# Four-model block on one core: softmax of negated scores with fewer reciprocals, and latent-attention queries of 96 columns a head

## The chip, the cores and the metric

The kernel runs on one core of a Trainium2 chip. The metric is device time in microseconds for one launch, which computes a whole stack of layers for 512 tokens of width 1024. The times of the kernel before are 1867.73, 1868.81 and 1868.92 us, median 1868.81 us.

## The reference, cut to what matters

Two blocks run one after the other. The first has a sparse-attention mixer (8 heads), a gated linear mixer and a feed-forward part. The second has four layers, each followed by a layer norm: latent attention (`_mla_branch`), sliding-window attention, attention with a forget gate (`_fox_branch`), and latent attention once more. The change touches the dense causal softmax, which the sparse mixer, the forget-gate layer and both latent layers use, and the queries and keys of the two latent layers:

```python
q = (_rmsnorm(cq, q_norm) @ w_q_up).reshape(B, S, 16, 64 + 32)
kv = (_rmsnorm(ckv, kv_norm) @ w_kv_up).reshape(B, S, 16, 64 + 64)
q_rope = _apply_rope(q[..., 64:], cos, sin)   # [x1*cos - x2*sin, x2*cos + x1*sin], halves of 16
k_rope = _apply_rope(k_rope, cos, sin)        # one, shared by all 16 heads
q_full = concat([q[..., :64], q_rope]);  k_full = concat([kv[..., :64], k_rope])
s = einsum(q_blk, k_full) * 96 ** -0.5;  s = where(causal, s, -1e30)
p = softmax(s);  o = einsum(p, v)             # swept over 128-query blocks
```

## The kernel before

Everything is computed in fp32 accuracy by splitting each operand into a high part (fp32r, made by ScalarE) and a low part (the rest, made by VectorE); a product of two split operands is three matmuls on TensorE: high by high, high by low and low by high (`mm3`, lines 268 to 277). The Python code is traced by a framework that then orders the instructions of each engine itself, by a simulated timeline and the buffers that its pools have: the program text sets what is computed and which buffers there are, and each engine then runs its own list strictly in order.

A latent layer (`mla`, from line 1107) first projects the tokens to the low-rank vectors (`cq`, 384 wide, and `ckv`, 256 wide) and transposes them to feature-major tiles `ct`. It then loops over four quads of four heads. For a quad it loads and splits the query weights, the key and value weights and the gate weights, projects the gates (`pj<-Ah,wh` in the rows) and the values (`vt`, four token blocks), and then takes two pairs of heads. For a pair it projects the keys of both heads at once (a matmul group with 128 features and 512 tokens, `pj<-cth,wh`), splits each half into the tiles `k4h` and `k4l`, and projects each head's query in a group of its own, again of 128 features: 64 plain features, 32 rotary ones, and the same 32 once more with the two halves swapped, so that the rotation needs one multiplication by a table (`tab`, line 1204) whose rows hold cos, cos, -sin, sin; the sum over features then adds the products. The keys carry the rotated key on both sets of 32 rows. The three matmuls of each of a query projection's three feature chunks are nine matmuls of 512 columns. The query is then split into `qh` (ScalarE, line 218) and `ql` (VectorE, line 219), both of which read the projection's PSUM bank `pj`. There are three such banks, two `s` banks for scores and two `t` banks for transposes.

`dense_head` (line 316) takes the four query blocks of a head. For each block TensorE makes the scores; VectorE adds the mask and takes the row maximum in one instruction (L324), negates it (L326, one column); ScalarE takes the exponential and the row sum (L327); VectorE takes the reciprocal (L328, one column) and scales the block (L331). TensorE then transposes the blocks (L337), ScalarE copies the transposes out (`pt`, L205), and `dense_values` multiplies them with the values of both heads of the pair into the one bank `o` (L350), which VectorE multiplies by the gate into `og` (L1103). `og` has eight tiles of 512 columns, two a quad.

In the rows `wl<-wr,wh` and `wh<-wr` are weight splits, `sp` the scores, `mx` and `nm` the maximum and its negative, `sum` and `rc` the row sum and its reciprocal. VectorE is DVE, ScalarE is ACT, GpSimd POOL, SyncE SP; TensorE is PE, its weight loads PEld.

## Time and profile before

| what | value |
|---|---|
| median of three runs | 1868.81 us |
| the profiled execution: its own time, and its span from first to last instruction | 1871.75 us, 1870.0 us |
| granted TensorE clock, mean | 0.997 |
| TensorE, VectorE, ScalarE busy share | 97%, 65%, 49% |
| first latent layer, four quads (890 to 1064 us) | 174 us |
| second latent layer, four quads (1655 to 1830 us) | 175 us |
| forget-gate layer, four quads (1350 to 1573 us) | 223 us |

The busy time of a matmul in the rows contains its way through the array, so that neighbours overlap; what a matmul costs in a dense row is the distance from its start to the next one's. A bracket at the end of a row gives the idle time of the engine just before it and what ended it.

### The profile page before, as it was taken

How to read it: one execution, taken by the hardware profiler on the slowest of the kernel's cores; microseconds unless marked ns; L12 is line 12 of the kernel's file. 1: busy time of each engine (PE TensorE's matmuls, PEld its weight loads, DVE VectorE, ACT ScalarE, POOL GpSimd, SP SyncE). 2: the span in 40 equal slices, each digit the busy share in tenths (PEclk: the TensorE clock that was granted, in tenths of full speed). 3: DMA queues.
4: the chain of work that ended last, by engine and by line, in shares of the span. 5: the costliest groups of instructions: out<-in, count | busy, mean ns of one | idle time of the engine just before them, and what ended most of it. 6: DMA issues, size and time to landing. Idle time of an engine off the chain costs nothing.

```text
span 1870.0 us, 27371 instructions
## 1 busy us (share of the span) xinstructions
PE 1822.0 (97%) x10155; PEld 1498.8 (80%) x10155; DVE 1223.9 (65%) x3055; ACT 907.1 (49%) x2030; POOL 166.6 (9%) x217
## 2 busy tenths in 40 slices
PE   7999999999999999999999999999999999999997
PEld 7877777678888888879887788877888877988775
DVE  5554387754954664556878675576776666787866
ACT  4543336743442442344667434463566564366651
POOL 2211200000200000001000011241000000200001
PEclk9999999999999999999999999999999999999999
DMA  7222141042332342324221133221432322232111
GB/s 217 80 58 57 36 127 40 26 139 79 91 106 75 102 132 81 91 76 108 58 71 57 47 104 91 70 64 38 113 80 54 83 69 79 75 87 59 47 56 46
DMA packets 200752, 148.14 MB, mean 79 GB/s; under 512 B 8765, under 2 KB 178538, under 8 KB 200618
## 3 DMA queue, kind: packets, MB, share of 16 engines
q1 hardware_dynamic: 198826, 140.97, 26.3%
q0 software_dynamic: 1792, 5.42, 0.9%
q8 instruction: 80, 1.31, 0.3%
q14 instruction: 54, 0.44, 0.1%
HBM read 144.27 MB, written 2.10 MB: 78 GB/s over the span
## 4 chain that ended last, share of the span: by engine, by line
PE 67%; DVE 4%; ACT 2%; issue 1%; POOL 0%; POOLq 0%; DVEq 0%; ACTq 0%
PE pj L273 17%; PE pj L275 17%; PE pj L276 16%; PE o L350 3%; PE pj L937 3%; PE t L337 3%; PE s L937 1%; DVE wl L215 1%; PE s L275 1%; PE s L273 1%; PE s L276 1%; PE t L937 1%; PE t L372 1%; PE t L1319 1%; PE s L1419 1%
## 5 line engine op out<-in xcount | busy, mean ns | idle before, releaser
L214 ACT ACTIVATE wh<-wr 128x1024 fp32r<-128x1024 f32 (+10 forms) x408 | 296.0, 755 | 408.7 <-PE pj L275 130.9
L215 DVE TENSOR_TENSOR wl<-wr,wh 128x1024 fp32r<-128x1024 f32 (+10 forms) x408 | 344.0, 866 | 215.2 <-ACT wh L214 210.5
L273 PE MATMUL pj<-Ah,wh 128*128 128x512 f32 (+1 forms) x944 | 370.6, 393 | 4.8 <-DVE fg L288 2.8
L275 PE MATMUL pj<-Al,wh 128*128 128x512 f32 (+1 forms) x944 | 369.0, 391 | 0.2 <-DVE Al L215 0.2
L276 PE MATMUL pj<-Ah,wl 128*128 128x512 f32 (+1 forms) x944 | 368.1, 391 | 0.0
L273 PE MATMUL pj<-wh,Ah 128*128 128x512 f32 (+5 forms) x640 | 219.0, 343 | 4.7 <-ACT Ah L214 4.6
L275 PE MATMUL pj<-wl,Ah 128*128 128x512 f32 (+5 forms) x640 | 216.6, 339 | 0.0
L276 PE MATMUL pj<-wh,Al 128*128 128x512 f32 (+5 forms) x640 | 214.8, 340 | 0.5 <-DVE Al L215 0.4
L273 PEld LDWEIGHTS pj<-Ah,wh 128*128 128x128 f32 x944 | 178.1, 189 | 42.4 <-DVE fg L288 3.2
L276 PEld LDWEIGHTS pj<-Ah,wl 128*128 128x128 f32 x944 | 178.2, 189 | 37.4 <-issue 1.5
L275 PEld LDWEIGHTS pj<-Al,wh 128*128 128x128 f32 x944 | 178.1, 189 | 35.6 <-issue 0.8
L327 ACT ACTIVATE sp<-sp,nm 128x128 f32<-128x128 f32 (+3 forms) x256 | 142.8, 559 | 75.5 <-DVE nm L326 73.4
L205 ACT ACTIVATE pt<-t 128x512 f32<-128x512 f32 (+3 forms) x288 | 115.1, 444 | 106.1 <-PE t L337 66.8
L324 DVE CUSTOM_DVE_ANT_0 sp<-s,c_causal 128x128 f32<-128x128 f32 (+3 forms) x256 | 121.1, 486 | 56.7 <-PE s L276 23.5
L273 PEld LDWEIGHTS pj<-wh,Ah 128*128 128x128 f32 x640 | 121.4, 190 | 19.6 <-ACT Ah L214 7.3
L276 PEld LDWEIGHTS pj<-wh,Al 128*128 128x128 f32 x640 | 120.9, 190 | 12.6 <-DVE Al L215 1.6
L275 PEld LDWEIGHTS pj<-wl,Ah 128*128 128x128 f32 x640 | 121.5, 190 | 10.9 <-issue 0.2
L337 PE MATMUL t<-ident,sp 128*128 128x128 f32 x640 | 108.9, 278 | 5.1 <-ACT pt L205 5.0
L337 PEld LDWEIGHTS t<-ident,sp 128*128 128x128 f32 x640 | 77.3, 140 | 30.8 <-ACT pt L205 12.7
L331 DVE TENSOR_SCALAR sp<-sp,rc 128x128 f32<-128x128 f32 (+3 forms) x256 | 96.7, 383 | 5.0
L273 PE MATMUL pj<-wh,hdh 128*128 128x512 f32 x176 | 69.1, 393 | 3.3 <-ACT fg L205 2.2
L275 PE MATMUL pj<-wl,hdh 128*128 128x512 f32 x176 | 68.6, 390 | 0.0
(474 smaller groups left out, 3304.4 us busy)
## 6 DMA issues: line engine op xcount, KB each, us to landing
wr<-in_w_in_dram SPq DMA_DIRECT2D x34, 512.0 KB, 3.9
wr<-in_fox_w_in_dram SPq DMA_DIRECT2D x30, 512.0 KB, 4.1
wr<-in_w_ffn_gate_dram SPq DMA_DIRECT2D x22, 512.0 KB, 4.2
wr<-in_w_ffn_up_dram SPq DMA_DIRECT2D x22, 512.0 KB, 3.8
wr<-in_w_ffn_down_dram SPq DMA_DIRECT2D x22, 512.0 KB, 3.6
wr<-in_swa_w_in_dram SPq DMA_DIRECT2D x20, 512.0 KB, 3.8
wr<-in_mla_w_in_dram SPq DMA_DIRECT2D x16, 512.0 KB, 4.0
wr<-in_mla_w_out_dram SPq DMA_DIRECT2D x16, 512.0 KB, 3.8
```

Of the source, the lines that this page charges most:

```text
L205: return self.nc.scalar.activation(out, in_, AF.Copy, scale=1.0 if scale is None else scale)
L214: self.nc.scalar.activation(h, src, AF.Copy)
L215: self.nc.vector.tensor_tensor(out=l, in0=src, in1=h.bitcast(F32), op=ALU.subtract)
L273: mm = self.nc.tensor.matmul(ps, lhsT=ah, rhs=bh, start=i == 0, stop=False)
L275: self.nc.tensor.matmul(ps, lhsT=ah, rhs=bl, start=False, stop=False)
L276: mm = self.nc.tensor.matmul(ps, lhsT=al, rhs=bh, start=False, stop=i == n - 1)
L324: nc.vector.tensor_tensor_reduce(out=v, in0=ps, in1=self.causal[:, S - n:S], scale=1.0, scalar=LOWEST, op0=ALU.add, op1=ALU.max, accum_out ...
L327: nc.scalar.activation(v, v, AF.Exp, bias=nm[:, g], accum_out=sm[:, g])
L331: nc.vector.tensor_scalar(v, v, rc[:, g], None, ALU.mult)
L337: nc.tensor.transpose(ps[:, (b - j) * 128:(b - j + 1) * 128], sp[:, POFF[b] + j * 128:POFF[b] + j * 128 + 128], self.ident)
L350: mm = self.nc.tensor.matmul(po[64 * i:64 * i + 64, j * 128:S], lhsT=value(j, i), rhs=pt[:, TOFF[j]:TOFF[j] + (NB - j) * 128], start=first ...
L937: nc.tensor.matmul(ps, lhsT=x, rhs=y, start=first and k == 0 and i == 0, stop=last and k == 3 and i == 2, skip_group_check=True)
```

## The change

In `dense_head` the instruction that masks the scores now writes their negative and takes the row minimum, so that the negated maximum comes out of it directly and the separate negation goes; the exponential gets a scale of -1. The reciprocals of the first three blocks are taken in one instruction of three columns after the third block's row sum is there, and their three scalings follow it; the fourth block has its own.

In `mla` a quad's queries now take three projections of 128 features, where they took four. The first two, one for each head of the first pair, hold that head's 64 plain features, its 32 rotary features, and the 32 rotary features of the head at the same place in the second pair. The third holds the plain features of both heads of the second pair. No feature is projected twice: a query's rotary features x enter the scores as x cos and x sin, 32 rows each, and the keys carry the rotated key on the first 32 and its swapped and signed form on the second 32. For a head of the first pair VectorE therefore makes four products on 32 rows each out of the projection (new line 1221): two into a tile `qf` for the head of the second pair, two in place in the bank. For the second pair ScalarE copies the plain features into `qf`, and the split reads `qf`. `qf` lies in tiles 6 and 7 of `og` in the first three quads; in the fourth it is a third tile of the two-buffer pool `vt`. The query weights of a quad come in seven column ranges in place of two, and are split by two wide instructions on each of ScalarE and VectorE in place of fourteen narrow ones.

```diff
@@ dense_head
             nc.vector.tensor_tensor_reduce(
-                out=v, in0=ps, in1=self.causal[:, S - n:S], scale=1.0, scalar=LOWEST, op0=ALU.add, op1=ALU.max, accum_out=mx[:, g])
-            nc.vector.tensor_scalar(nm[:, g], mx[:, g], -1.0, None, ALU.mult)
-            nc.scalar.activation(v, v, AF.Exp, bias=nm[:, g], accum_out=sm[:, g])
+                out=v, in0=ps, in1=self.causal[:, S - n:S], scale=-1.0, scalar=-LOWEST, op0=ALU.add, op1=ALU.min, accum_out=nm[:, g])
+            nc.scalar.activation(v, v, AF.Exp, bias=nm[:, g], scale=-1.0, accum_out=sm[:, g])
+            if b < NB - 2:
+                continue
+
+            done = range(NB - 1) if b == NB - 2 else (b,)
+            g = slice(done[0], b + 1)
             nc.vector.reciprocal(rc[:, g], sm[:, g])
...
-            nc.vector.tensor_scalar(v, v, rc[:, g], None, ALU.mult)
+            for c in done:
+                v = sp[:, POFF[c]:POFF[c] + (c + 1) * 128]
+                nc.vector.tensor_scalar(v, v, rc[:, c:c + 1], None, ALU.mult)
@@ mla, keys: 32 + 32 rows, the second 32 swapped and signed
-                    for r0 in (0, 32, 64, 96):
-                        nc.vector.tensor_tensor(out=kr[:, b, r0:r0 + 32], in0=t[:, 0:32], in1=t[:, 32:64], op=ALU.add)
...
+                    nc.vector.tensor_tensor(out=kv[:, :, 0:32], in0=tv(0, 32), in1=tv(32, 32), op=ALU.add)
+                    nc.vector.tensor_tensor(out=kv[:, :, 32:48], in0=tv(16, 16), in1=tv(48, 16), op=ALU.add)
+                    nc.vector.scalar_tensor_tensor(out=kv[:, :, 48:64], in0=tv(0, 16), scalar=-1.0, in1=tv(32, 16), op0=ALU.mult, op1=ALU.subtract)
@@ mla, query weights
-                for pr in range(2):
-                    v = self.wload(wqu, 0, 3, (quad * 384 + pr * 192, 192))
-                    h, l = self.wtile(3, 256)
...
+                for ranges in (((0, 96), (256, 32), (160, 32), (352, 32), (96, 64)), ((192, 64), (288, 64))):
+                    v = self.wload(wqu, 0, 3, *((o + c, n) for c, n in ranges))
+                    h, l = self.wtile(3, v.shape[-1])
+                    self.split_into(h, l, v)
@@ mla, queries
+                    if pr == 0:
+                        room = og[:, KD - 2:KD] if quad < 3 else l2.tile([128, NB, 256], F32, name="vt").rearrange("p (h c) n -> p h (c n)", h=2)
+                        qf = [room[:, hh] for hh in range(2)]
+                    else:
+                        ps = self.pj()
+                        self.proj_feat(ps, qw[1], cq, kc=3)
+                        for hh in range(2):
+                            r = slice(64 * hh, 64 * hh + 64)
+                            self.acopy(qf[hh][r], ps[r], 96 ** -0.5)
                     for hh in range(2):
-                        ps = self.pj()
-                        self.proj_feat(ps, qw[pr], cq, kc=3, cols=slice(hh * 128, hh * 128 + 128))
-                        r = slice(64 - 64 * hh, 128 - 64 * hh)
-                        nc.vector.tensor_tensor(out=ps[r], in0=ps[r], in1=tab[r], op=ALU.mult)
                         q = [l2.tile([128, S], F32R, name=n) for n in ("qh", "ql")]
-                        self.split_gain(*q, ps, scale[:, hh:hh + 1])
+                        if pr == 0:
+                            ps = self.pj()
+                            self.proj_feat(ps, qw[0], cq, kc=3, cols=slice(hh * 128, hh * 128 + 128))
+                            own, other = (slice(64 - 64 * hh + c, 96 - 64 * hh + c) for c in (0, 32))
+                            for out, src, tab in ((qf[hh][own], other, cos), (qf[hh][other], other, sin), (ps[other], own, sin), (ps[own], own, cos)):
+                                nc.vector.tensor_tensor(out=out, in0=ps[src], in1=tab[src], op=ALU.mult)
+                            self.split_gain(*q, ps, scale[:, hh:hh + 1])
+                        else:
+                            self.split_into(*q, qf[hh])
```

Over the whole program this takes 72 matmuls of 512 columns from TensorE (24 of each of the three kinds). The framework orders all engines anew. Three places matter below.

**VectorE, first quad of the first latent layer**, from the first rotation on; `pj` here is the bank of a projection, `k4l` the low part of a key, `wl` a weight split for the next quad, `ql` the low part of the query. Before:

```order
L1204 TENSOR_TENSOR pj<-pj,c_mla_tab 64x512
L215 TENSOR_TENSOR k4l<-pj,k4h 64x512
L219 SCALAR_TENSOR_TENSOR ql<-pj,scale,qh 128x512
L1204 TENSOR_TENSOR pj<-pj,c_mla_tab 64x512
L215 TENSOR_TENSOR wl<-wr,wh 128x1024
L219 SCALAR_TENSOR_TENSOR ql<-pj,scale,qh 128x512
```

The first query's low part stands third in this list, the second query's sixth. The same place in the changed program:

```order
L1221 TENSOR_TENSOR og<-pj,c_mla_cos 32x512
L1221 TENSOR_TENSOR og<-pj,c_mla_sin 32x512
L211 TENSOR_TENSOR k4l<-pj,k4h 64x512
L1221 TENSOR_TENSOR pj<-pj,c_mla_sin 32x512
L1221 TENSOR_TENSOR og<-pj,c_mla_cos 32x512
L1221 TENSOR_TENSOR og<-pj,c_mla_sin 32x512
L1221 TENSOR_TENSOR pj<-pj,c_mla_cos 32x512
L211 TENSOR_TENSOR wl<-wr,wh 128x1024
L1221 TENSOR_TENSOR pj<-pj,c_mla_sin 32x512
L211 TENSOR_TENSOR wl<-wr,wh 128x1024
L211 TENSOR_TENSOR k4l<-pj,k4h 64x512
L215 SCALAR_TENSOR_TENSOR ql<-pj,scale,qh 128x512
```

The first query's low part now stands twelfth: seven of the eight products, both weight splits and two key splits are ahead of it.

**VectorE, second quad of the first latent layer**, between the second head's products and the first head's low part (`sp,nm<-s` is the masked minimum of a score block, the `nm` row under it reads its result out, `og<-o` is the gate of the pair before). Before, the matching place has one product for each head:

```order
L1204 TENSOR_TENSOR pj<-pj,c_mla_tab 64x512
L215 TENSOR_TENSOR k4l<-pj,k4h 64x512
L324 ISA sp,mx<-s,c_causal 128x256
L324 ISA mx 128x1
L219 SCALAR_TENSOR_TENSOR ql<-pj,scale,qh 128x512
```

After, the low part comes behind two more weight splits, a key split and the gate:

```order
L1221 TENSOR_TENSOR og<-pj,c_mla_sin 32x512
L321 ISA sp,nm<-s,c_causal 128x128
L321 ISA nm 128x1
L321 ISA sp,nm<-s,c_causal 128x256
L321 ISA nm 128x1
L1221 TENSOR_TENSOR pj<-pj,c_mla_cos 32x512
L211 TENSOR_TENSOR wl<-wr,wh 128x1024
L1221 TENSOR_TENSOR pj<-pj,c_mla_sin 32x512
L211 TENSOR_TENSOR wl<-wr,wh 128x1024
L211 TENSOR_TENSOR k4l<-pj,k4h 64x512
L1106 SCALAR_TENSOR_TENSOR og<-o,og 128x512
L215 SCALAR_TENSOR_TENSOR ql<-pj,scale,qh 128x512
```

Ahead of this piece stand three more products, the first two of either head's and one in the bank.

**VectorE, fourth quad of the first latent layer.** Before, its first rotation stands among the blocks of the third quad's last heads, 33 rows of the list ahead of the gate `og<-o` of the third quad's second pair:

```order
L215 TENSOR_TENSOR k4l<-pj,k4h 64x512
L1204 TENSOR_TENSOR pj<-pj,c_mla_tab 64x512
L215 TENSOR_TENSOR k4l<-pj,k4h 64x512
L324 ISA sp,mx<-s,c_causal 128x384
L324 ISA mx 128x1
```

After, all eight products follow that gate in one run, since `qf` is here a `vt` tile whose buffer the third quad's values hold until the matmuls of `o` have read them:

```order
L211 TENSOR_TENSOR k4l<-pj,k4h 64x512
L329 RECIPROCAL rc<-sum 128x1
L334 TENSOR_SCALAR sp<-sp,rc 128x512
L211 TENSOR_TENSOR wl<-wr,wh 128x1024
L1106 SCALAR_TENSOR_TENSOR og<-o,og 128x512
L1221 TENSOR_TENSOR vt<-pj,c_mla_cos 32x512
L1221 TENSOR_TENSOR vt<-pj,c_mla_sin 32x512
L1221 TENSOR_TENSOR vt<-pj,c_mla_cos 32x512
L1221 TENSOR_TENSOR vt<-pj,c_mla_sin 32x512
L1221 TENSOR_TENSOR pj<-pj,c_mla_sin 32x512 x2
L1221 TENSOR_TENSOR pj<-pj,c_mla_cos 32x512 x2
L215 SCALAR_TENSOR_TENSOR ql<-pj,scale,qh 128x512 x2
```

Both query projections of the fourth quad are made before that gate and hold two of the three `pj` banks until these rows are done.

## Rows read from the trace of the kernel before

**Rows 1.** Page: engine, busy us (share of the span) x instructions.
```profile
PE 1822.0 (97%) x10155; PEld 1498.8 (80%) x10155; DVE 1223.9 (65%) x3055; ACT 907.1 (49%) x2030; POOL 166.6 (9%) x217
```
**Rows 2.** Windows of the two latent layers' quads: width, PE, PEld, DVE, ACT busy.
```profile
890.00:1064.00 174.00, 171.86 (x951) 136.51 (x952) 135.12 (x447) 111.36 (x295) 1.15 (x2) 1.00 0.19 57
1655.00:1830.00 175.00, 172.23 (x952) 136.68 (x953) 135.48 (x447) 112.41 (x297) 1.15 (x2) 1.00 0.18 54
```
**Rows 3.** Timeline, first quad of the first latent layer: start us, us, instruction.
```profile
891.98 0.40 PE L273 MATMUL pj<-cth,wh 128*128 128x512 f32 x1
...
894.08 0.39 PE L273 MATMUL pj<-cth,wh 128*128 128x512 f32 x1
...
894.28 0.71 DVE L1204 TENSOR_TENSOR pj<-pj,c_mla_tab 64x512 f32<-64x512 f32 x1 [0.20 <-PE pj L276]
...
895.02 0.69 ACT L218 ACTIVATE qh<-pj,scale 128x512 fp32r<-128x512 f32 x1 [0.91 <-DVE pj L1204]
...
895.74 0.75 DVE L219 SCALAR_TENSOR_TENSOR ql<-pj,scale,qh 128x512 fp32r<-128x512 f32 x1
...
897.58 0.22 PE L273 MATMUL s<-k4h,qh 128*128 128x128 f32 x1
...
898.03 0.39 PE L276 MATMUL s<-k4h,ql 128*128 128x128 f32 x2
898.27 0.39 PE L273 MATMUL pj<-cth,wh 128*128 128x512 f32 x1
...
904.22 0.47 PE L273 MATMUL pj<-Ah,wh 128*128 128x512 f32 x1 [0.38 <-DVE k4l L215]
```
**Rows 4.** Groups by shape on DVE, 840 to 1095 us: busy, mean ns of one.
```profile
L215 DVE TENSOR_TENSOR wl<-wr,wh 128x1024 fp32r<-128x1024 f32 x19 | 23.0, 1217 | 1.9 <-ACT wh L214 1.7
L219 DVE SCALAR_TENSOR_TENSOR ql<-pj,scale,qh 128x512 fp32r<-128x512 f32 x16 | 11.9, 743 | 0.8 <-ACT qh L218 0.8
L1204 DVE TENSOR_TENSOR pj<-pj,c_mla_tab 64x512 f32<-64x512 f32 x16 | 11.2, 700 | 2.0 <-PE pj L276 1.7
L215 DVE TENSOR_TENSOR k4l<-pj,k4h 64x512 fp32r<-64x512 f32 x16 | 11.0, 686 | 1.2 <-ACT k4h L214 1.0
...
L328 DVE RECIPROCAL rc<-sum 128x1 f32<-128x1 f32 x64 | 10.0, 158 | 6.4 <-ACT sp L327 5.8
L326 DVE TENSOR_SCALAR nm<-mx 128x1 f32<-128x1 f32 x64 | 9.0, 145 | 0.4
...
L324 DVE CUSTOM_DVE_ANT_0 sp<-s,c_causal 128x256 f32<-128x256 f32 x16 | 6.7, 418 | 1.2 <-PE s L276 1.2
...
L324 DVE CUSTOM_DVE_ANT_0 sp<-s,c_causal 128x128 f32<-128x128 f32 x16 | 4.5, 283 | 4.8 <-PE t L337 2.7 <-PE s L276 2.1
...
L1103 DVE SCALAR_TENSOR_TENSOR og<-o,og 128x512 f32<-128x512 f32 x6 | 4.1, 688 | 0.8 <-PE o L350 0.7
```
**Rows 5.** Timeline at a pair's end in the second latent layer.
```profile
1826.16 0.60 PE L337 MATMUL t<-ident,sp 128*128 128x128 f32 x4
...
1827.34 0.71 PE L337 MATMUL t<-ident,sp 128*128 128x128 f32 x3 [0.58 <-ACT pt L205]
...
1828.42 2.37 PE L350 MATMUL o<-pt,vt 128*64 128x512 f32 x16 [0.37 <-ACT pt L205]
```
**Rows 6.** What TensorE waited for in the sparse mixer's attention, 270 to 400 us.
```profile
PE t L337 <- ACT pt L205: 2.1, 7, 0.6
PE s L311 <- DVE mx L324: 1.4, 5, 0.4
```
**Rows 7.** Windows in the feed-forward part; third figure from the right: granted clock.
```profile
502.00:505.47 3.47, 1.68 (x12) 1.35 (x11) 3.47 (x4) 0.41 (x1) 0.00 (x0) 1.00 0.46 137
505.47:508.88 3.41, 3.41 (x10) 2.64 (x9) 3.41 (x5) 0.63 (x1) 0.00 (x0) 0.50 0.54 157
```
**Rows 8.** Timeline of SyncE's issues and a split: the next quad's query weights.
```profile
898.49 0.37 SPq L236 DMA_DIRECT2D wr<-in_mla_w_q_up_dram  x1
...
902.63 1.39 ACT L214 ACTIVATE wh<-wr 128x288 fp32r<-128x288 f32 x7
```

More of the change, by code (lines that the diff above doesn't have):

```diff
@@ L87, in shape_constants @@
     sc = np.float32(96 ** -0.5)
-    tab = np.empty((128, S), np.float32)
-    for base in (0, 64):
-        tab[base:base + 16] = tab[base + 16:base + 32] = cos.T * sc
-        tab[base + 32:base + 48], tab[base + 48:base + 64] = -sin.T * sc, sin.T * sc
-    out["mla_tab"] = tab
+    out["mla_cos"], out["mla_sin"] = np.tile(cos.T * sc, (8, 1)), np.tile(sin.T * sc, (8, 1))
     kr = np.concatenate([cos, cos, -sin, sin], axis=1)
@@ L317, in dense_head @@
         sp = P.tile([128, 1280], F32, name="sp", bufs=bufs)
-        mx, nm, sm, rc = (self.sm(NB, n) for n in ("mx", "nm", "sum", "rc"))
+        nm, sm, rc = (self.sm(NB, n) for n in ("nm", "sum", "rc"))
         for b in range(NB):
@@ L1111, in mla @@
             l1 = c1.enter_context(tc.tile_pool(name="l1", bufs=1))
-            tab = self.load_const(l1, "mla_tab")
+            cos, sin = self.load_const(l1, "mla_cos"), self.load_const(l1, "mla_sin")
             scale = l1.tile([128, 2], F32, name="scale")
@@ L1138, in mla @@
                     nc.vector.tensor_tensor(out=t[:, 48:64], in0=ps[:, 256:272], in1=kro[:, b, 48:64], op=ALU.mult)
-                    for r0 in (0, 32, 64, 96):
-                        nc.vector.tensor_tensor(out=kr[:, b, r0:r0 + 32], in0=t[:, 0:32], in1=t[:, 32:64], op=ALU.add)
+                    kv = kr[:, b].rearrange("p (u c) -> p u c", u=2)
+                    tv = lambda o, n: t[:, None, o:o + n].to_broadcast([128, 2, n])
+                    nc.vector.tensor_tensor(out=kv[:, :, 0:32], in0=tv(0, 32), in1=tv(32, 32), op=ALU.add)
+                    nc.vector.tensor_tensor(out=kv[:, :, 32:48], in0=tv(16, 16), in1=tv(48, 16), op=ALU.add)
+                    nc.vector.scalar_tensor_tensor(out=kv[:, :, 48:64], in0=tv(0, 16), scalar=-1.0, in1=tv(32, 16), op0=ALU.mult, op1=ALU.subtract)
                 for c in range(6):
@@ L1159, in mla @@
             for quad in range(4):
-                qw = []
-                for pr in range(2):
-                    v = self.wload(wqu, 0, 3, (quad * 384 + pr * 192, 192))
-                    h, l = self.wtile(3, 256)
-                    for u in range(2):
-                        r, s0 = 64 - 64 * u, u * 96
-                        pieces = ((0, 0, 96),) if u == 0 else ((192, 0, 64), (128, 64, 32))
-                        for d, c, n in pieces + ((128 * u + r + 32, 80, 16), (128 * u + r + 48, 64, 16)):
-                            self.split_into(h[:, :, d:d + n], l[:, :, d:d + n], v[:, :, s0 + c:s0 + c + n])
+                o, qw = quad * 384, []
+                for ranges in (((0, 96), (256, 32), (160, 32), (352, 32), (96, 64)), ((192, 64), (288, 64))):
+                    v = self.wload(wqu, 0, 3, *((o + c, n) for c, n in ranges))
+                    h, l = self.wtile(3, v.shape[-1])
+                    self.split_into(h, l, v)
                     qw.append(Split([(0, 3, h, l)]))
```

## The prediction

> **What bounds the kernel now.** The page's engine line comes first: TensorE is busy for 1822.0 of 1870.0 us, VectorE for 65% [rows 1]. So what counts is matmuls taken away, and every microsecond for which TensorE is made to wait. The windows then show how far this holds where the change works: in the two latent layers' quads TensorE is busy for 171.86 of 174 and 172.23 of 175 us, VectorE for only 135 [rows 2]. There is hardly a wait to shorten there; what can be won is matmuls alone. The timeline of the first quad shows how the cover works [rows 3]: a query's projection starts at 891.98 and is over, by its ninth successor, at 894.08. The rotation follows at 894.28, the low part is ready at 895.74 + 0.75 = 896.49, and TensorE, which has other projections until 897.58, reaches the score matmul that reads it at 898.03. The slack is 1.5 us. VectorE has spare time on the average and little here, and that is what I follow below.
>
> **TensorE: matmuls taken away.** Nine matmuls take 894.08 - 891.98 = 2.10 us, 0.233 each [rows 3]. The 72 that go are nine a quad in eight quads: 72 x 0.233 = 16.8 us, all of it in saturated time. The changed program's projections, scores and transposes are otherwise the same, so without new waits the quads would shorten by that.
>
> **VectorE: the products.** The trace has no operation on 32 rows. The nearest row is the one on 64 rows, 700 ns; the gate of the same 512 columns on 128 rows takes 688 [rows 4]. Twice the rows cost nothing more, so I take 0.70 us for a product on 32 rows; were the time proportional to rows below 64, it would be 0.35, and an upper bound is the 743 of the low part, which has a third operand. A query of a first pair had one such operation and now has four; a query of a second pair has none. In sum 32 x 0.70 go and 64 x 0.70 come: 22 us more over both layers, against which stand the softmax savings below and fewer, wider weight splits. VectorE is at 135 of 174 us and has room; the price comes from where the products stand.
>
> The Trainium skill, "VectorE: DVE Perf Modes", section "Why `tensor_reduce` can't reduce along partition axis", says that each of the 128 partition lanes is a pipeline of its own and the data stream along the free dimension. By that 32 rows save nothing, and the sum would keep 0.70; the two rows above agree with it between 64 and 128, and none in this trace shows 32.
>
> **First quad of each latent layer.** Nothing runs before it to cover it. From the first query's end VectorE has, in the order shown, seven products, two key splits, two weight splits and the low part: 7 x 0.700 + 2 x 0.686 + 2 x 1.217 + 0.743 = 9.45 us [rows 4]. From 894.28 [rows 3] that is 903.7, and with the 0.2 that TensorE takes to follow 903.9. TensorE's own list there is the second query, a key projection and the high-part scores, all done at 898.0, as before. The low-part scores that stood at 898.03 move to 903.9: 5.9 us of waiting. Behind it one query projection is saved (2.1), and the present wait of 0.38 before the gate projection [rows 3], in all with its neighbour 0.5, goes since its key is long split. Net +3.3; for both layers +6.6. With products at 0.35 the low part comes 2.45 us earlier, and net is +0.9 each.
>
> **Second and third quads.** Here the pair before is still at work and covers more. In the second quad of the first layer VectorE has from the first query's end six products (4.2), two key splits (1.37), the minima of two blocks (0.283 + 0.418, and some 0.08 each to read the result, an estimate from half of the one-column operation's 145), two weight splits (2.43), the gate (0.69) and the low part (0.74): 10.3 us [rows 4]. TensorE meanwhile has the second query (2.1), a key projection (1.4), the `o` matmuls (2.4, [rows 5]) and some 2.3 of scores and transposes, 8.2 us, then the third projection, whose bank is the first query's and is free only with that low part. Wait: 2.1, just what the projection saves. By the same count I find about 2 for the next quad, and 1.5 and 0 in the second layer, where the lists are looser. Waits 5.6 against 4 x 2.1 saved: -2.8. With products at 0.35 no wait is left: -8.4.
>
> **Fourth quads.** `qf` is a third `vt` tile, so no product can be written before the third quad's last `o` has read its values. Both query banks stay taken and the keys and the third projection share the remaining one. I count: 0.75 for the key projection that waits for that bank; 2.1 for the third projection behind the key's split, with 8 products (5.6) and the gate on VectorE; about 0.95, since the transposes and `o` of the pair before stand without cover, as the end of a layer shows now (0.58 + 0.37, [rows 5]); 1.4 for the gate projection, which waits for two ScalarE copies of the size of `qh` (0.69 each, [rows 3]). That is 5.2 less 2.1 saved: +3.1 a layer, +6.2 for both. I hold -1 to +5 a layer possible, since these four waits may partly cover one another.
>
> **Softmax.** In 64 heads, 32 of them in the latent layers, the negations go (four a head, 145 ns) and of four reciprocals of 158 ns two stay [rows 4]: 0.9 us of VectorE a head. It was not the bound in most of them. Where TensorE waited for this chain, in the sparse mixer, 2.1 us went to `pt` copies and 1.4 to the maximum [rows 6]. With the forget-gate layer's I take 2.5 us off. Bounds: 3.5 off, and 2 on, since three blocks are now scaled after the third sum and their transposes come later in a bunch.
>
> **Loads.** Five more query-weight loads a quad and two tables for one: 42 issues of 0.37 us on SyncE, which only issues. The next quad's weights are issued at 898.49 and split at 902.63, long before the quad that reads them begins [rows 8]. I cost it at nothing; without that cover it is 5 x 0.37 = 1.9 a quad.
>
> **The clock.** In the feed-forward part TensorE was busy for 1.68 of 3.47 us, one wait of 1.8; in the following 3.41 us the granted clock was 0.50, 1.2 GHz, and TensorE went through that stretch at half speed [rows 7]. That is 1.7 us on top of a wait. The waits of the first and fourth quads are as long or longer. There are four such places; I take two falls, +3.4, bounds 0 and 6.8. The Trainium skill, "TensorE: Matmul & The Clock Gate", section "What's actually happening", says that the slow clock is the default and activity releases it; this speaks against the change's first quads, and by it every one of the four could fall, which would make it +6.8.
>
> **Sum.** +6.6 - 2.8 + 6.2 - 2.5 + 3.4 = +10.9, against the profiled execution's 1871.75 us: 1882.7. That execution lies 2.9 above the median 1868.81, so the median to expect is 1879.7, say 1879.5.
>
> **Rivals.**
> - *The products are over early, faster.* Place: VectorE between a first pair's query and its low part. If a product on 32 rows costs about 0.35, the numbers above give +1.8 (first quads) - 8.4 + 0.6 (fourth, where eight products shrink by 2.8) - 2.5 = -8.5: 1860. With no new wait at all it would be -16.8 - 2.5, 1849.5. It decides from about 0.45 us a product on. For it: VectorE is a quarter idle [rows 2]. Against it: 64 and 128 rows cost alike. 0.24.
> - *The waits eat the saving, no more.* The fourth quads' waits overlap (+1 a layer), the clock stays up: 6.6 - 2.8 + 2 - 2.5 = +3.3, 1872. About the bound of 0.2%, 3.7 us, either side. 0.17.
> - *Waits and clock together.* All four places fall to the slow clock (+6.8) and the second and third quads lose a further 1 us each: 1879.7 + 3.4 + 4 = 1887, up to 1893 where the loads lose their cover too. For it [rows 7]; against, other projections lie between the waits. 0.11.
> - *Forecast.* 0.48, its own range 1873 to 1885.
>
> **Numbers.** Faster by over 0.2% (3.7 us, what a measurement of this kernel can tell): the first rival and a little of the second, 0.26. Within: 0.16. Slower: the forecast, the third and the rest, 0.58. The range that should hold 8 in 10 reaches from 1857, in the first rival, to 1889.
>
> **What would show it.** In the changed profile: products of 32x512 at about 700 ns; in each first quad TensorE idle for 4 to 6 us before a score matmul of `k4h,ql`, ended by VectorE's `ql`; in the fourth quads several waits for a `pj` bank and one of the gate projection for ScalarE; spells of clock 0.50 behind them. Quads one and four longer than before, two and three shorter. Products of 350 ns, or TensorE still busy for 99% of the latent windows, would make the forecast wrong on the fast side; so would a first quad whose low part is done before 900.

## The result

The changed kernel takes 1889.65 us (four runs, 1888.7 to 1892.47) against 1868.87: ratio 1.0113, 95% interval 1.01 to 1.0125. That is 20.8 us slower where 10.7 were forecast (1879.5 against 1868.81), and 0.65 us beyond the range. The profiled execution is one of 1892.47 us.

The page's engine line of the changed kernel, to be held against [rows 1]: engine, busy us (share of the span) x instructions.

```profile
PE 1818.4 (96%) x10083; PEld 1492.9 (79%) x10083; DVE 1191.6 (63%) x2567; ACT 903.8 (48%) x1950; POOL 166.1 (9%) x217
```

The 72 matmuls are gone, yet TensorE's busy time fell by 3.6 us, not by 16.8; the matmuls that are left kept it busy for longer, in part at a lower clock, and the span grew by 20.5. VectorE has 488 instructions and 32 us less. The windows of the two latent layers' quads (width, PE, PEld, DVE, ACT busy, ..., granted clock third from the right), for [rows 2]:

```profile
888.00:1074.00 186.00, 170.13 (x920) 132.87 (x919) 133.61 (x347) 113.73 (x281) 1.16 (x2) 0.98 0.18 54
1663.00:1852.00 189.00, 172.54 (x922) 134.36 (x923) 134.16 (x348) 113.44 (x283) 1.15 (x2) 0.97 0.18 50
```

The quads take 186 and 189 us where they took 174 and 175. TensorE idles for 16 us in each where it idled for 2 to 3, and the clock is 0.98 and 0.97 where it was 1.00. VectorE is busy for as long as before, 134 us: it is not its sum that changed but where its work stands. The first quad's timeline, for [rows 3]:

```profile
891.96 0.69 DVE L1221 TENSOR_TENSOR og<-pj,c_mla_cos 32x512 f32<-32x512 f32 x1 [0.20 <-PE pj L272]
...
894.12 0.71 DVE L1221 TENSOR_TENSOR pj<-pj,c_mla_sin 32x512 f32<-32x512 f32 x1
...
896.27 0.70 DVE L1221 TENSOR_TENSOR pj<-pj,c_mla_cos 32x512 f32<-32x512 f32 x1
...
897.00 1.23 DVE L211 TENSOR_TENSOR wl<-wr,wh 128x1024 fp32r<-128x1024 f32 x1
897.25 0.67 ACT L214 ACTIVATE qh<-pj,scale 128x512 fp32r<-128x512 f32 x1
897.97 0.33 PE L269 MATMUL s<-k4h,qh 128*128 128x128 f32 x1 [2.10 <-ACT qh L214]
...
898.87 1.20 DVE L211 TENSOR_TENSOR wl<-wr,wh 128x1024 fp32r<-128x1024 f32 x1
...
900.60 0.73 DVE L215 SCALAR_TENSOR_TENSOR ql<-pj,scale,qh 128x512 fp32r<-128x512 f32 x1
...
901.39 0.80 PE L272 MATMUL s<-k4h,ql 128*128 128x128 f32 x2 [2.69 <-DVE ql L215]
901.98 0.63 PE L269 MATMUL pj<-cth,wh 128*128 128x512 f32 x1
```

From the first product at 891.96 to the end of the low part at 901.33 VectorE works without a pause for 9.4 us, the 9.45 of the sum. TensorE waits 2.10 us for the high part, which I had not seen (it too has to wait for the products in the bank), and 2.69 for the low part. The last row is the third effect: a matmul of 512 columns takes 0.63 us, at the clock's lower level (granted clock 0.50, 1.2 GHz), for 0.40. The products by form on VectorE, 840 to 1095 us (busy, mean ns), for [rows 4]:

```profile
L1221 DVE TENSOR_TENSOR pj<-pj,c_mla_sin 32x512 f32<-32x512 f32 x8 | 5.6, 700 | 0.2
...
L1221 DVE TENSOR_TENSOR og<-pj,c_mla_sin 32x512 f32<-32x512 f32 x6 | 4.1, 690 | 0.1
```

Thirty-two rows cost 700 and 690 ns, what 64 cost before. Then what TensorE waited for in the first latent layer's quads (us in total, times, longest), in the changed kernel:

```profile
PE t L340 <- ACT pt L201: 4.7, 8, 1.1
PE s L272 <- DVE ql L215: 2.7, 1, 2.7
PE pj L269 <- DVE ql L215: 2.6, 2, 1.7
PE s L269 <- ACT qh L214: 2.1, 1, 2.1
PE pj L269 <- ACT vt L201: 1.3, 1, 1.3
```

and in the kernel before:

```profile
PE t L337 <- ACT pt L205: 0.9, 2, 0.6
PE pj L273 <- DVE k4l L215: 0.4, 1, 0.4
PE o L350 <- ACT pt L205: 0.4, 1, 0.4
```

By what ended them, the new waits for `ql` are the largest, 2.7 and 2.6 us. The largest row is one that I had for the fourth quads alone: transposes that wait for ScalarE's copies of earlier ones, 4.7 us where it was 0.9. By quad, from a quad's first projection of 512 columns to the next quad's (the fourth: to the layer norm's first statistics), in us:

| quad | before, layers 1 and 2 | changed | difference |
|---|---|---|---|
| first | 33.4, 33.4 | 38.9, 38.6 | +5.5, +5.2 |
| second | 40.6, 40.1 | 40.9, 40.5 | +0.3, +0.4 |
| third | 32.2, 32.7 | 32.6, 33.4 | +0.4, +0.7 |
| fourth | 71.3, 71.8 | 75.8, 78.0 | +4.4, +6.2 |

Together +23.0 (summed before rounding). The rest of the program is 2.5 us shorter. That is about what the softmax gains alone (below), but that it is the softmax there is not shown.

### The profile page after: what moved, and what is told of

It is laid out like the page before. It is cut to its first block, busy times and chain, and to the rows that moved or that the text cites. A ratio compares the mean times of both kernels' runs of the same rounds, so it can differ in the third digit from the quotient of the medians.

```text
span 1890.5 us, 26791 instructions
## 1 busy us (share of the span) xinstructions
PE 1818.4 (96%) x10083; PEld 1492.9 (79%) x10083; DVE 1191.6 (63%) x2567; ACT 903.8 (48%) x1950; POOL 166.1 (9%) x217
## 3 DMA queue, kind: packets, MB, share of 16 engines
q8 instruction: 79, 1.29, 0.3%
## 4 chain that ended last, share of the span: by engine, by line
PE 64%; DVE 6%; ACT 3%; issue 2%; POOL 0%; POOLq 0%; DVEq 0%; ACTq 0%
PE pj L269 16%; PE pj L271 16%; PE pj L272 16%; PE pj L940 3%; PE o L353 2%; PE t L340 2%; DVE wl L211 1%; PE s L940 1%; ACT pt L201 1%; PE s L272 1%; PE s L269 1%; PE s L271 1%; DVE og L1221 1%; PE t L940 1%; DVE pj L1221 1%
## 5 line engine op out<-in xcount | busy, mean ns | idle before, releaser
L210 ACT ACTIVATE wh<-wr 128x1024 fp32r<-128x1024 f32 (+8 forms) x312 | 284.4, 922 | 406.7 <-PE pj L271 139.9
L211 DVE TENSOR_TENSOR wl<-wr,wh 128x1024 fp32r<-128x1024 f32 (+8 forms) x312 | 332.0, 1076 | 221.8 <-ACT wh L210 219.6
L323 ACT ACTIVATE sp<-sp,nm 128x128 f32<-128x128 f32 (+3 forms) x256 | 142.6, 559 | 71.3 <-DVE nm L321 69.8
L334 DVE TENSOR_SCALAR sp<-sp,rc 128x128 f32<-128x128 f32 (+3 forms) x256 | 86.7, 383 | 2.9
```

Source lines behind the costliest of these rows:

```text
L210: self.nc.scalar.activation(h, src, AF.Copy)
L211: self.nc.vector.tensor_tensor(out=l, in0=src, in1=h.bitcast(F32), op=ALU.subtract)
L323: nc.scalar.activation(v, v, AF.Exp, bias=nm[:, g], scale=-1.0, accum_out=sm[:, g])
L334: nc.vector.tensor_scalar(v, v, rc[:, c:c + 1], None, ALU.mult)
```

## The experiments

Every run was timed against the kernel before on its own chip, so the ratios are compared; "us" behind a ratio is its difference to 1 times 1868.8. On that scale the changed kernel is +21.1.

**The two parts apart.** First the new `dense_head` in the kernel before, then the old one in the changed kernel:

```diff
-out=v, in0=ps, ..., scale=1.0, scalar=LOWEST, op0=ALU.add, op1=ALU.max, accum_out=mx[:, g])
+out=v, in0=ps, ..., scale=-1.0, scalar=-LOWEST, op0=ALU.add, op1=ALU.min, accum_out=nm[:, g])
+done = range(NB - 1) if b == NB - 2 else (b,)      # and on; e2 takes these edits back in the changed kernel
```

> The kernel before with only the new softmax (negated minimum, reciprocals of three blocks at once). Theory A (the new waits of the changed kernel's latent quads all come from the query products on VectorE): the sparse mixer keeps its gain of about 2.3 us, the latent quads stay as in the kernel before: 1866 us, 1864.5 to 1867.5. Theory B (the three scalings in a bunch make the transposes late in the latent quads, so that the softmax part has a share in the loss): 1870 to 1874 us.

Measured: 1867.23 against 1870.13, ratio 0.9985 (0.9976 to 0.9993), -2.8 us. The number is theory A's, the place is not. In the sparse mixer (270 to 400 us) TensorE waits no less than in [rows 6]:

```profile
PE s L311 <- DVE nm L325: 2.5, 9, 0.4
PE t L344 <- ACT pt L205: 1.7, 4, 0.9
```

The latent quads, which were to stay as they were, are 1.1 and 0.7 us shorter in the profile (176.4 for 177.5, 177.3 for 178.1).

> The changed kernel with the softmax of before. Theory A: it loses the softmax gain and nothing else, 1889.65 + 2.5 = 1892 us, 1890.5 to 1894. Theory B (the softmax part has a share in the latent quads' loss): 1880 to 1887 us, since the waits for ScalarE's transposed copies in the latent quads would go back towards those of before.

Measured: 1894.87, 1.0131 (1.0117 to 1.0145), +24.5. Theory A both times: the softmax gains about 3 us in either kernel and has no share in the loss. Theory B falls.

**The fourth quad's tile.**

```diff
-room = og[:, KD - 2:KD] if quad < 3 else l2.tile([128, NB, 256], F32, name="vt")...
+room = og[:, KD - 2:KD]
```

> The changed kernel with the fourth quad's second-pair queries in og tiles 6 and 7 as in the other quads, not in a third tile of vt. Theory A (the fourth quads lose 5.3 us a layer because the products wait for the third quad's values and hold two of three banks): most of that comes back, 8 us in all, 1881.5 us, 1879 to 1884. Theory C (the fourth quads lose because 18 projections less are left there to cover the end of the third quad): 1887 to 1890 us.

Measured: 1907.71, 1.0198 (1.0184 to 1.0213). The edit changes more than it was meant to: in the fourth quad the first pair's output is copied into `og` tile 6, so the second pair's first query is read only after that copy has overwritten it (that head's query is not the reference's), and the fourth quads, which now wait for that copy, are 8.5 and 7.1 us longer than the changed kernel's in the profile. It tells nothing of the two theories; the next run has the tile right.

```diff
+cs = self.load_const(l1, "mla_cs"); spare = l1.tile([128, S], F32, name="spare")  # one table, rows cos 32, sin 32, ...
+qf = [og[:, KD - 2] if quad < 3 else spare, og[:, KD - 1]]
```

> The changed kernel with one table of cos and sin in alternating 32 rows, and, in the space that this frees, a tile of their own for the fourth quad's second-pair queries (one in og tile 7, one in a tile of 512 columns): the products of the fourth quad need not wait for the third quad's values. Theory A (that wait, with two of three banks held, makes the fourth quads 5.3 us a layer longer): 8 us come back, 1881.5 us, 1878 to 1885. Theory C (the fourth quads lose for want of other work beside the third quad's end): 1887 to 1890 us.

Measured: 1889.56 (1882.57 to 1890.61), 1.0105 (1.0089 to 1.0121). By the median theory C, but the runs tell more. Three of the four are at 1888.6 to 1890.6 with a mean clock of 0.991 or 0.992, one is at 1882.57 with 0.995; the changed kernel has 0.994 and 0.995. In the profile the fourth quads are 1.8 and 3.8 us shorter, but at waits of 2.0 and 2.2 us for a row minimum that now stand there the clock falls (0.73 over 1015 to 1020 us, 0.71 over 1790 to 1795), and in the second and third quads it falls twice more (0.66 over 945 to 950, 0.68 over 1765 to 1770).

```diff
+twice = quad == 3      # four projections, rotary features projected twice, ps[r] *= cs[r] on 64 rows, no qf
```

> The changed kernel with four query projections in the fourth quad alone: each head's rotary features are projected twice, one product of 64 rows by a table of cos and sin rows, no qf tile there (18 matmuls more in both layers, 4.2 us). Theory A (the fourth quads' loss of 5.3 us a layer comes from their products and from the wait for the value tile): 10.6 us come back, 1879 us, 1876 to 1882. Theory C (it comes from elsewhere, so that the run with a tile of its own could not mend it): 1887 to 1894 us.

Measured: 1888.87, 1.0096 (1.0078 to 1.0114), clock 0.992. By the median theory C. As in the run before, the profile says more: 2.2 and 3.7 us less in the fourth quads, with 4.2 of matmuls more; of that 3.2 us show in the ratio (+17.9 for +21.1), and the intervals overlap.

**The products.**

```diff
+nc.gpsimd.memset(qf[hh][64 - 64 * hh:128 - 64 * hh], 0.125)
-for out, src, tab in ((qf[hh][own], other, cos), (qf[hh][other], other, sin), (ps[other], own, sin), (ps[own], own, cos)):
+for out, src, tab in ((ps[other], own, sin), (ps[own], own, cos)):
```

> The changed kernel without the two products a head that go to the second pair's queries (their rotary rows are a constant, written by GpSimd). Theory A (VectorE's time on the products makes the waits): 2 to 3 products fewer ahead of each first low part, first quads 2.5 us shorter each, second and third 1.5 each, fourth 2 each, one fall of the clock less: 1889.65 - 5 - 6 - 4 - 1.7 = 1873 us, 1869 to 1878. Theory D (the waits come from bank reuse and the order, whatever the products take): 1884 to 1890 us.

Measured: 1860.27 against 1870.13, 0.9946 (0.9931 to 0.9961), -10.1 us. Theory A, and more than it said: leaving out 32 products of 0.70 us, 22 us of VectorE, takes 31 us off the time, and the mean clock is back at 0.998. In three parts, by the quads in which the two products are left out:

```diff
+if quad == 0:          # e13     if quad in (1, 2):  # e14     if quad == 3:  # e15
```

> As the run with two products (1860.27), but the two products a head are left out in the first quad of each layer alone (constants from GpSimd there). Theory A (the loss is local to each quad): the first quads get back the 8 us each by which they are longer than in that run, half of it clock: 1889.65 - 15 = 1874.5 us, 1872 to 1878. Theory G (VectorE's delay is handed on from quad to quad, so that only leaving all out helps): 1884 us or more.

> The same in the second and third quads alone. Theory A: 1.4 to 2.7 us a quad, 7 in all: 1882.5 us, 1880 to 1885. Theory G: 1887 us or more, or below 1878 if the delay of the fourth quads is handed on from these.

> The same in the fourth quad alone. Theory A: 4.1 and 4.9 us, 1881 us, 1879 to 1884. Theory H (the waits of the fourth quads go, but falls of the clock at the waits that are left take it back, as 0.991 against 0.994 in the run with a tile of its own): 1886 to 1890 us with a lower mean clock than the changed kernel's 0.994.

Measured: 1.0078 (1.0064 to 1.0092), 1.0060 (1.0047 to 1.0074) and 1.0068 (1.0054 to 1.0082): -6.5, -9.9 and -8.4 us against the changed kernel, -24.8 in sum where all at once gave -31. So every quad has a share in the loss. The intervals, some 2.6 us either way, do not rank the three runs, and the second and third are two quads a layer. Some of the loss is handed on: with the first quads mended by 8.1 and 6.4 us in the profile, the second and third became 1.9 and 2.7 us longer together. Theory A holds for the middle and fourth quads, where theory H falls; for the first quads the result stands at theory G's 1884, far from theory A's 1874.5. In the stretch of the second and third quads (927 to 1003 us) the changed kernel's TensorE waits for

```profile
PE pj L269 <- DVE ql L215: 2.6, 2, 1.7
PE t L340 <- ACT pt L201: 1.5, 3, 0.7
```

and the run with two products there waits for

```profile
PE t L340 <- ACT pt L201: 1.0, 2, 0.8
```

**The products without the change.** The kernel before keeps its four projections and gets products that nobody reads, in the first three quads:

```diff
+if pr == 0 and quad < 3:
+    for out, src in ((lo, lo), (hi, hi), (lo, hi)):      # e12: only the first
+        nc.vector.tensor_tensor(out=og[out, KD - 2 + hh], in0=ps[src], in1=tab[src], op=ALU.mult)
 nc.vector.tensor_tensor(out=ps[r], in0=ps[r], in1=tab[r], op=ALU.mult)
```

> The kernel before with three products on 32 rows more for each query of a first pair in the first three quads, written to og tiles that nobody reads: no matmul is taken away, only VectorE's list ahead of the low part is made like that of the changed kernel (36 products, 25 us of VectorE over both layers). Theory A (such products make TensorE wait): first quads +5 and the clock's 1.7, second and third quads +1.5 each: 1870 + 19 = 1889 us, 1880 to 1895. Rival (VectorE has room, the products cost only where projections were taken away): 1870 to 1874 us.

Measured: 1895.14 against 1868.71, 1.0140 (1.0124 to 1.0155), +26.2. The two waits of the changed kernel's first quad (2.7 and 2.1 us there) are here with no matmul taken away, and in the second quad stands one of 3.3 for a row maximum (first latent layer):

```profile
PE s L273 <- DVE mx L324: 3.3, 1, 3.3
PE s L276 <- DVE ql L219: 2.5, 1, 2.5
PE s L273 <- ACT qh L218: 2.1, 1, 2.1
```

> The kernel before with one product on 32 rows more for each first-pair query in the first three quads, where the earlier run had three (12 products, 8.4 us of VectorE). Theory A (the low part has some 1.5 us of slack, so that the first products are free and the later ones dear): 1869 to 1872 us. Theory F (every product costs 0.73 us of the end, 26.4 for 36): 1877.5 us, 1875 to 1880.

Measured: 1873.55 against 1869.32, 1.0021 (1.0011 to 1.003), +3.9. That is between the two theories. The first product of each query costs 0.33 us of the end (12 of them), the next two 0.93 (24, +22.3): there is some slack ahead of the low part, and it is used up quickly. But a good part of the 0.93 is the clock. The first quad, then the second and third, of the first layer, with three products and then with one (granted clock third from the right):

```profile
888.05:928.48 40.43, 35.61 (x178) 29.33 (x176) 32.33 (x98) 22.48 (x62) 0.00 (x0) 0.92 0.20 54
928.48:1008.15 79.67, 74.11 (x420) 58.46 (x419) 67.19 (x214) 48.28 (x133) 0.00 (x0) 0.98 0.17 51
```

```profile
886.68:921.17 34.49, 33.34 (x176) 27.82 (x174) 29.01 (x95) 22.87 (x63) 0.00 (x0) 1.00 0.23 64
921.17:993.77 72.60, 71.95 (x419) 57.19 (x418) 60.96 (x206) 46.73 (x131) 0.00 (x0) 1.00 0.20 56
```

The second layer has the same, 0.92 and 0.98 against 1.00 and 1.00. What is missing from a clock of 1.00, times the widths, is 9.7 us in both layers, an estimate of the clock's part of the +26.2; without it the next two products cost some 0.5 us each.

**Off VectorE.** ScalarE copies the second pair's rotary features out of the bank, and one late product a head, on 64 rows, goes to GpSimd or stays on VectorE:

```diff
+self.acopy(qf[hh][own], ps[other]); self.acopy(qf[hh][other], ps[other])
+nc.gpsimd.tensor_tensor(out=qf[hh][r], in0=qf[hh][r], in1=cs[r], op=ALU.mult)   # pr == 1; e7: nc.vector
```

> As the run with a tile of its own, and the second pair's rotary features leave the bank as two ScalarE copies of 32 rows a head; GpSimd multiplies them by the table later, in one operation of 64 rows a head. VectorE has two products a head ahead of the low part instead of four. Theory A (products on VectorE are the cause, as the run with two products shows with 1860.27): 1866 us, 1861 to 1870, since the copies lie ahead of the high part on ScalarE. Theory E (ScalarE's copies take the products' place as the wait): 1875 to 1885 us.

Measured: 1862.66 (1858.84 to 1863.19), 0.9962 (0.9949 to 0.9974), -7.1. Theory A. The five runs lie in two groups: two at 1858.8 with a mean clock of 0.998, three at 1862.7 to 1863.2 with 0.996.

> As the run before it, with the late product on VectorE instead of GpSimd: 16 operations of 0.70 us a layer more on VectorE, of which none stands ahead of a first pair's low part. Theory A (what counts is what stands ahead of the low part, not VectorE's sum): within 3 us of the GpSimd version, 1866 to 1869. Theory F (VectorE's sum counts): half of what the two products cost comes back, about 1875 us.

Measured: 1877.04, 1.0047 (1.0033 to 1.006), +8.8. Theory F's number: 16 operations (in both layers together, not in each), 11.2 us, cost 15.9. But these stand ahead of the second pair's low parts, which I had overlooked, so the run doesn't tell VectorE's sum from the place. The next does:

```diff
+twice = True
```

> The changed kernel with four query projections in every quad, projected twice as in the run before it: what is left of the change is the softmax, the swap on the keys' side and two wide weight splits for fourteen narrow ones. Theory A (what stands ahead of a low part counts, VectorE's sum does not): as the softmax alone, 1867.2 us on the scale of before at 1870.1, that is 0.9985 of before, 1864 to 1867.5. Theory F (VectorE's sum counts, at about 0.9 us of the end for 1 us of VectorE): some 15 us of narrow splits go, 1853 to 1858.

Measured: 1869.35 against 1869.32, 0.9995 (0.9986 to 1.0004). Theory F falls: twelve narrow splits a quad less on VectorE bring nothing that can be measured. Its 15 us were too many, for VectorE is busy for 1174.2 us where the softmax alone leaves it 1181.8, 7.6 less; but at 0.9 each even these would have shown. The softmax says the same: 42 us less of VectorE (1181.8 for 1223.9) gained 2.8. Theory A's 0.9985 is missed too, by 1.9 us, and why is open. So in these runs it is not VectorE's sum that counts but what stands between a projection and a query's low part.

```diff
+twice = quad == 0      # on the GpSimd version
```

> The version with the late product on GpSimd (1862.66), with four projections in the first quad of each layer alone, where its trace still shows a wait of 1.44 us and a fall of the clock (1.7 us). Theory A: these 3.1 us a layer go, 2.1 of matmuls come back: 1860.5 us, 1858 to 1863. Rival (the saved matmuls count in full, the wait is covered elsewhere): 1866 us.

Measured: 1868.57, 0.9992 (0.9983 to 1.0001). Slower than the GpSimd version by 5.6 us, more than the 4.2 of its matmuls; the wait of 1.44 is gone from the first quads (32.8 us each), but the second ones are longer, 40.5 and 41.3 us for 37.9 and 37.2. Neither theory said that.

**The clock by itself.** The GpSimd version with work that nobody needs in the first quads' wait:

```diff
+fill = self.pso()      # first quad, behind the second query's projection
+for _ in range(6):
+    nc.tensor.matmul(fill, lhsT=ct[0][:, 0, 0:128], rhs=ct[0][:, 1], start=True, stop=True)
```

> The version with the late product on GpSimd (1862.66), with six matmuls of 512 columns into the idle output bank, whose result nobody reads, behind the second query's projection in the first quad of each layer, where TensorE waits for 1.44 us: 2.8 us of matmuls more in both layers. Theory H (the wait is filled at no cost and the clock does not fall, 1.7 us a layer): 1859 us, 1857.5 to 1860.5. Rival (the work simply adds, or the clock falls all the same): 1862.5 to 1866 us.

Measured: 1859.7 (1859.47 to 1861.66), 0.9943 (0.993 to 0.9957), -10.7: theory H's number. But the intervals of the two versions overlap, and two of the five runs without the six matmuls (1858.8) are faster than any with them (1859.47 at best). The medians don't show a gain, so the step is read from the profiles. Without the six matmuls TensorE waits and then runs at 0.63 us a matmul:

```profile
899.47 0.33 PE L269 MATMUL s<-k4h,qh 128*128 128x128 f32 x1 [1.44 <-ACT qh L214]
...
900.89 0.63 PE L271 MATMUL pj<-ctl,wh 128*128 128x512 f32 x1
```

With them it is on at the same scores 0.3 us earlier, and the same projection runs at 0.40:

```profile
896.14 1.53 PE L1223 MATMUL o<-cth 128*128 128x512 f32 x6
...
899.16 0.33 PE L269 MATMUL s<-k4h,qh 128*128 128x128 f32 x1
...
900.56 0.40 PE L271 MATMUL pj<-ctl,wh 128*128 128x512 f32 x1
```

The windows of 898 to 908 us, first with a clock of 0.79 and 0.87 (GpSimd version), then 1.00 (padded):

```profile
898.00:903.00 5.00, 3.45 (x13) 2.70 (x13) 4.91 (x9) 3.99 (x8) 1.26 (x1) 0.79 0.19 39
903.00:908.00 5.00, 5.00 (x21) 4.12 (x20) 3.83 (x10) 3.84 (x8) 0.00 (x0) 0.87 0.40 116
```

```profile
898.00:903.00 5.00, 4.81 (x24) 3.67 (x23) 4.91 (x11) 4.17 (x8) 1.29 (x1) 1.00 0.22 44
903.00:908.00 5.00, 5.00 (x23) 3.89 (x22) 4.90 (x13) 4.24 (x11) 0.00 (x0) 1.00 0.66 197
```

The first quads go from 34.3 us to 32.9 each. That the clock stays up there is shown; that the whole kernel gains is not. In the padded profile the clock falls between the third and the fourth quad of the first layer instead, where the GpSimd version has 1.00:

```profile
1003.60:1007.10 3.50, 3.50 (x14) 1.24 (x14) 2.26 (x8) 1.45 (x6) 0.00 (x0) 0.55 0.38 133
```

and the two profiled executions are 1.5 us apart (1861.66 and 1863.19). The padded version has the lowest ratio of those that leave nothing out, 0.57% below the kernel before.

## Why the prediction was wrong in its size

*Direction and mechanism were right.* VectorE's list ahead of the first low part took 9.4 us for the 9.45 summed, products on 32 rows cost 0.70, and two of the waits stand where they were put, the low part's in the first quads and the gate projection's in the fourth. The run that adds the products to the kernel before makes that a shown cause, and the run that leaves two out takes it away. The Trainium skill's rule ("VectorE: DVE Perf Modes", section "Why `tensor_reduce` can't reduce along partition axis"), lanes that work independently, agrees with the 700 and 690 ns on 32 rows.

*The clock, +3.4: mis-sized.* I took two falls of 1.7 us. The changed kernel's profile has, behind the first quad's waits:

```profile
898.00:903.00 5.00, 2.31 (x9) 1.92 (x10) 4.88 (x8) 1.28 (x2) 0.00 (x0) 0.79 0.49 135
903.00:908.00 5.00, 5.00 (x14) 3.89 (x13) 2.07 (x6) 2.90 (x7) 0.00 (x0) 0.53 0.02 9
901.39:907.72 6.33, 6.33 (x16) 5.07 (x17) 3.62 (x8) 3.59 (x8) 0.00 (x0) 0.50 0.23 79
```

TensorE works from 901.39 on at half the clock until about 907.7, nearly twice the length of [rows 7]. That costs 3.1 us if half of it is lost, and 2.9 by the distance from one matmul to the next (0.43 us for 0.23). It is the same in the second layer's first quad (0.57 over 1675 to 1680, 0.75 over 1680 to 1685), with one spell of 3.4 us in its last (0.66 over 1795 to 1800). That is 3.1 + 3.1 + 1.7 = 7.9 us, above the upper bound of 6.8 that I had for all four places. Three of these four show a fall, and two of the falls are about twice as long as I had priced. I had weighed the Trainium skill's rule ("TensorE: Matmul & The Clock Gate", section "What's actually happening"), which has the slow clock as the default, too lightly.

*Second and third quads, -2.8: the step that failed.* I set 5.6 us of waits, all for a low part's bank, against 8.4 saved. Measured +1.8. The waits for `ql` are there, and smaller than that sum (2.6 us in the first layer, 1.1 in the second). What I had put at nothing stands behind them: minima late for the score banks (0.9, 0.3 and 0.4 us in the second layer's third quad), scalings late for the transposes, and these then in a bunch waiting for ScalarE's copies (1.5 in the first layer). Two of these rows:

```profile
1753.74 0.30 PE L340 MATMUL t<-ident,sp 128*128 128x128 f32 x1 [0.55 <-DVE sp L334]
...
1761.38 0.30 PE L269 MATMUL s<-k4h,qh 128*128 128x128 f32 x1 [0.91 <-DVE nm L321]
```

The first layer's second and third quads (width, TensorE busy) in the kernel before, in the changed one, and with the two products a head left out there alone:

```profile
923.98:996.75 72.77, 72.19 (x421) 57.40 (x419) 59.46 (x204) 48.14 (x132) 0.00 (x0) 1.00 0.19 55
927.12:1000.59 73.47, 69.27 (x400) 54.24 (x400) 58.61 (x155) 49.90 (x124) 0.00 (x0) 1.00 0.21 59
927.66:996.46 68.80, 67.79 (x401) 54.02 (x401) 53.19 (x148) 48.87 (x125) 1.04 (x2) 1.00 0.23 63
```

TensorE idles for 0.6, 4.2 and 1.0 us. Without those products the stretch is 4.0 us shorter than before, nearly the 4.2 of its saved matmuls, so the products are what takes the saving away; in both layers 9.9 us come back. I had priced the first waiter behind the products and not the ones behind it. Not all of it is a wait that the profile names: idle time grew by 6.7 us in both layers, and the difference to the saving is 10.2 (8.4 and 1.8).

*Fourth quads, +6.2: mis-sized.* +10.6 measured, 1.7 of it the clock. Of my four waits, the two for a `pj` bank (0.75 and 2.1) stand in neither layer's rows as a wait of TensorE. The gate projection's wait for ScalarE's copies behind `o` came as summed (1.4):

```profile
1025.57 1.20 ACT L201 ACTIVATE vt<-pj 64x512 f32<-64x512 f32 x2 [2.47 <-PE o L353]
...
1026.82 0.50 PE L269 MATMUL pj<-Ah,wh 128*128 128x512 f32 x1 [1.29 <-ACT vt L201]
```

The transposes without cover cost more than the 0.95 taken, as the wait ahead of the third query projection shows (1.09, and 0.64 and 0.37 behind it; 3.4 us in all in the second layer):

```profile
1017.76 0.71 PE L340 MATMUL t<-ident,sp 128*128 128x128 f32 x3 [1.09 <-ACT pt L201]
...
1022.07 0.71 PE L340 MATMUL t<-ident,sp 128*128 128x128 f32 x3 [0.64 <-ACT pt L201]
...
1023.15 2.37 PE L353 MATMUL o<-pt,vt 128*64 128x512 f32 x16 [0.37 <-ACT pt L201]
```

That the value tile is what holds them is shown only in the profile (1.8 and 3.8 us with a tile of their own); the ratio moves by 1.5 us, inside its interval, and why the clock falls more often in that run stays open. With the two products a head left out there 8.4 us come back (4.0 and 5.5 in the profile): the loss hangs on these products, but whether on their time or on their wait for the tile is not told apart.

*First quads, +6.6: somewhat too large.* +10.6 with the clock, about 4.4 without its 6.2. The low part is done at 901.33 and not at 903.7, since the first product starts 2.3 us earlier than I had it; TensorE's two waits are 4.8 us for the 5.9 summed, and 2.1 of them are for the high part, which I had not seen.

*Softmax, -2.5: right in its number, and by luck, since the place was wrong.* -2.8 alone, but I had taken most of it from the sparse mixer's waits, and these did not get shorter in sum (3.5 us before, 4.2 with the new softmax). *The loads at nothing: right.* They appear in no wait of TensorE.

*The rivals.* "Over early" needed products of 0.35; they cost 0.70. "Waits and clock together" comes nearest to what happened (three of its four falls, and 1.2 us more in each second and third quad for its 1): its 1887 is nearest, with a chance of 0.11, too low: the row with a clock of 0.50 lay beside waits shorter than those that I forecast.

In sum: first quads 4.4, middle 1.8, fourth 8.9, clock 7.9, softmax -2.8, together 20.2 of the 20.5 us by which the span grew. The quads' terms are read from the same profile, so that they add up proves nothing by itself; the runs above carry the causes.

## What to carry to other kernels

Price an operation by what stands behind it in its engine's list, not by that engine's busy share: at 63% busy, products ahead of the split that frees a bank cost up to 0.9 us of the end for 0.7 of VectorE, the clock's part included, while narrow splits elsewhere cost nothing that could be measured. When a saturated TensorE is made to wait, add what the clock takes after the wait; and before removing matmuls that cover such a chain, move the chain to an engine with room (here ScalarE and GpSimd, -28 us against the changed kernel). Filling the hole with matmuls kept the clock up, and what it is worth to the whole kernel is open.

## What the runs showed of the hardware

With six matmuls of 512 columns added to a wait of 1.44 us the first quad became shorter, not longer (32.9 us for 34.3), and the granted clock stayed at 1.00 where it had been 0.79 and 0.87. GpSimd's product on 64 rows of 512 columns took 1.29 us, and VectorE's, the same operation, 0.69. And VectorE's time on 512 columns is the same on 32 rows (690 to 700 ns) as on 64 (686 to 700) and 128 (688) [rows 4].
